# A two-layer decoder trunk on one core: the opening of layer 0, the ends of the residual and of the recurrent block, and the end of the kernel put in another order

## The chip, the cores and the metric

The kernel runs on one core of one Trainium2 chip. The metric is the device time of the whole program in microseconds (us). Before the change the median of three runs is 629.0 us (627.55 to 630.78). The weights stream in from HBM while the core computes; activations stay on the chip.

The five engines have their own instruction streams: PE (TensorE) multiplies matrices, DVE (VectorE) and ACT (ScalarE) do elementwise work, POOL (GpSimd) does a few copies, and SP (SyncE) issues the DMA transfers. PE results land in PSUM, all else in SBUF.

## The reference, cut to what matters

Batch 1, 256 positions, width 1024, float32. Two layers and a final norm:

```python
for l in range(2):
    hn  = rms_norm(h, mix_norm_g[l])
    mix = even_mixer(hn, ...) if l % 2 == 0 else odd_mixer(hn, ...)
    h   = h + mix
    h   = h + conv_ffn(rms_norm(h, ffn_norm_g[l]), ...)
return rms_norm(h, final_norm_g)

def even_mixer(x):   # layer 0: attention (8 x 64) beside gated linear attention (8 x 32 / 64)
    aq, ak, av, bq, bk, bv, bgk, bog = split(x @ w_in)
    o_a   = attention(rotary(aq), rotary(ak), av)             # causal within the 256 positions
    log_a = log_sigmoid(bgk @ w_gk2 + b_gk2) / 16             # gates of the linear attention
    o_b   = rms_norm(gla(bq * 32**-0.5, bk, bv, log_a), g) * silu(bog)
    return concat(o_a, o_b) @ w_out

def odd_mixer(x):    # layer 1: gated recurrence
    gate, xr = split(x @ w_in);  xr = causal_dwconv(xr, 4 taps)
    r, i = sigmoid(block_diag(w_a) xr + b_a), sigmoid(block_diag(w_x) xr + b_x)
    a = exp(-8 r softplus(-lam));  u = sqrt(1 - a*a) * (i * xr)
    h = scan(h_t = a_t h_(t-1) + u_t)
    return (h * gelu(gate)) @ w_out

def conv_ffn(x):     # up 1024 -> 6144, causal conv of 3 taps, u * gelu(g), down 3072 -> 1024
    u, g = split(causal_dwconv(x @ w_up, 3 taps));  return (u * gelu(g)) @ w_down
```

## The kernel before, in words

Activations lie with their channels on the 128 partitions and the 256 positions along the free axis. The residual stream h is one tile of 8 row groups (m = 0 to 7) of 128 channels. In the trace it reads `big`, the name of the buffer that it shares with the small vectors.

Every large product is done in three passes, for accuracy. A float32 operand is split into a high part of fewer bits (hi) and the rest (lo), and the product is hi·hi + hi·lo + lo·hi. The weights come in 204 chunks of 128 x 1024 (512 KB each). `issue_w` (line 120) starts the DMA of a chunk into a buffer `w`, of which there are four; ACT makes `wh` from it (line 135) and DVE makes `wl` = w − wh (line 136), and the buffer of chunk i is free for chunk i+4 when `wl` of i is done. `gemm` and `passes` (line 147) issue, for each of the 8 blocks of a chunk, three matmuls of 256 columns: wh with x hi, wh with x lo, wl with x hi. So each chunk costs ACT a wh, DVE a wl and PE 24 matmuls.

The same split is made of activations: `scaled_split` (lines 206, 207) writes X hi on ACT (`x`, an activation with the norm's gain) and X lo on DVE. The norm's 1/rms is not applied to X; it is multiplied into the products' results afterwards. `Norm.add` squares a row group (`sq`, ACT, line 173) and adds it up (`ssq`, DVE, line 180); `Norm.rstd` lets PE add over partitions (`nps`, line 188), takes the root on ACT and the reciprocal on DVE, and spreads the result with two PE transposes (line 194).

The opening of layer 0: SP issues the loads of the small vectors (`vec`), the gate weight (`wgk`), x in four pieces (`xT`), then chunks and constants. ACT and DVE make X; PE does the gate product `psg`, then the query product of the linear attention `psbq` (chunks 0 and 1), its key product `psbk` (2 and 3) and the projections of the attention `psa` (chunks 4 to 11). From psbq comes `qn`, and 16 copies on POOL (lines 387 and 390) spread it into the block forms q0 and q1; from psbk comes `kn` (DVE, line 395). DVE also makes the gates' running sums (`G`, three scans `cum`) and the factors `KR`, ACT their exponentials `E`, and DVE the products `qb` and `kb`.

`residual` (line 212) adds a product into a row group of h, squares it and splits it for the next layer. In the feed-forward block the down product `psd` of the last group (m = 7) ends the layer; the next layer's first product `psx` needs all 8 groups. In the recurrent block the function `finish` (lines 725 to 730) makes, for each of four pairs of row groups, h·gelu(gate) as hi (`r`, DVE, line 728), the same in float32 (`hh`, line 729) and lo (`r`, line 730); the product `psout` then runs over these pairs. At the end of the kernel the final norm's factor is spread by PE transposes and DVE multiplies the 8 row groups, two at a time (line 756), and SP issues four output transfers of 256 KB (line 757).

The order on each engine is set by the framework's scheduler from the program order, its own cost figures and explicit edges: `order(a, b)` makes b come after a. A list of hooks by chunk, `state["hooks"]`, lets an operation be put ahead of the wh ("h") or the wl ("l") of a given chunk. `bank` picks a PSUM tile by tag.

## Time and profile before

| | before |
|---|---|
| time, median of 3 runs | 629.0 us (627.55 to 630.78) |
| profiled execution | 628.5 us, of which the span of the profile is 626.7 us |
| PE busy | 609.1 us (97%), 5210 matmuls |
| weight loads of PE (beside its matmuls) | 594.1 us (95%) |
| DVE busy | 516.1 us (82%) |
| ACT busy | 404.2 us (64%) |
| POOL busy | 30.9 us (5%) |
| read from HBM | 109.0 MB, 176 GB/s over the span |

An engine's busy time is the time in which it executed something. Idle time is put down to what released the engine: "PE psx <- ACT x" says that a matmul into psx started when an ACT instruction that writes x had ended. The granted clock (PEclk) is the share of TensorE's full clock that it had; at 0.50 it ran at 1.2 instead of 2.4 GHz. Idle time costs something only on an engine that something later waits for; here PE is idle in few places, and these can be listed one by one.

### The profile page before, as it was taken

The page shows a single profiled execution, that of the slowest core. Times are in us where ns is not written, and L with a number is a line of the kernel's source. Part 1 is how long each engine was busy: PE and PEld are TensorE (multiplying, and loading weights), DVE is VectorE, ACT ScalarE, POOL GpSimd, SP SyncE. Part 2 cuts the span into 40 slices and gives each one's busy share as a digit, 9 for nine tenths or more (in the row PEclk, how much of TensorE's full clock was granted, in tenths as well). Part 3 has the DMA queues.
Part 4 walks back from the last instruction along what each step waited for, and adds up shares of the span by engine and source line. Part 5 has one row for each costly group of instructions (what it writes and reads, how often), then busy time and mean ns, then how long its engine had stood idle before and what let it go on. Part 6 is the DMA issues. An engine that isn't in the chain of part 4 may idle for free.

```text
span 626.7 us, 13053 instructions
## 1 busy us (share of the span) xinstructions
PE 609.1 (97%) x5210; PEld 594.1 (95%) x5210; DVE 516.1 (82%) x899; ACT 404.2 (64%) x654; POOL 30.9 (5%) x58
## 2 busy tenths in 40 slices
PE   8989999999999999999998999989999999999995
PEld 4989998999999999999998999989999999999994
DVE  6799984577999999988667859997999999986542
ACT  6796564666766677765456588966676667774310
POOL 7470000000000000000000000000000000000000
PEclk9999999999999999999999999999999999999997
DMA  8734621325755555555568504535655555556501
GB/s 306 259 105 168 210 94 68 135 101 172 235 202 202 199 202 187 192 196 198 191 219 293 177 2 167 204 137 184 220 207 201 199 202 187 187 199 202 198 5 68
DMA packets 31517, 110.91 MB, mean 177 GB/s; under 512 B 3648, under 2 KB 4192, under 8 KB 31456
## 3 DMA queue, kind: packets, MB, share of 16 engines
q1 hardware_dynamic: 31456, 110.07, 50.7%
q8 instruction: 41, 0.67, 0.4%
q14 instruction: 20, 0.16, 0.1%
HBM read 109.01 MB, written 1.05 MB: 176 GB/s over the span
## 4 chain that ended last, share of the span: by engine, by line
PE 87%; DVE 4%; DMA 4%; ACT 3%; issue 2%; SPq 0%; DVEq 0%; ACTq 0%
PE psu L147 42%; PE psd L147 17%; PE psout L147 6%; PE pst L147 4%; PE psgb L147 3%; DMA w<-w 3%; PE psx L147 3%; PE psog L147 2%; DVE wl L136 2%; PE psa L147 2%; PE psgt L147 2%; ACT wh L135 1%; PE psbq L147 1%; PE pl L463 1%; PE pss L520 1%
## 5 line engine op out<-in xcount | busy, mean ns | idle before, releaser
L135 ACT ACTIVATE wh<-w 128x1024 fp32r<-128x1024 f32 x204 | 214.3, 1060 | 141.9 <-PE psu L147 69.5
L136 DVE TENSOR_TENSOR wl<-w,wh 128x1024 fp32r<-128x1024 f32 x204 | 248.2, 1222 | 53.5 <-ACT wh L135 49.3
L147 PE MATMUL psu<-x,wh 128*128 128x256 f32 x1536 | 262.2, 276 | 0.0
L147 PEld LDWEIGHTS psu<-x,wh 128*128 128x128 f32 x1536 | 231.3, 188 | 0.0
L147 PE MATMUL psu<-x,wl 128*128 128x256 f32 x768 | 211.7, 276 | 0.0
L147 PEld LDWEIGHTS psu<-x,wl 128*128 128x128 f32 x768 | 144.1, 188 | 0.0
L147 PE MATMUL psd<-y,wh 128*128 128x256 f32 x768 | 130.5, 276 | 0.0
L147 PEld LDWEIGHTS psd<-y,wh 128*128 128x128 f32 x768 | 115.5, 188 | 0.0
L147 PE MATMUL psd<-y,wl 128*128 128x256 f32 x384 | 105.4, 276 | 0.0
L645 DVE SCALAR_TENSOR_TENSOR c<-v,big,c 128x255 f32<-128x255 f32 (+1 forms) x192 | 83.8, 477 | 0.0
L147 PEld LDWEIGHTS psd<-y,wl 128*128 128x128 f32 x384 | 71.9, 188 | 0.0
L643 ACT ACTIVATE c<-v,big 128x256 f32<-128x256 f32 x96 | 51.7, 587 | 1.0 <-DVE y L650 0.6
L638 DVE TENSOR_TENSOR v<-psu,rs 128x512 f32<-128x512 f32 x48 | 32.6, 684 | 0.0
L173 ACT ACTIVATE sq<-big 128x256 f32<-128x256 f32 x40 | 15.3, 404 | 25.3 <-DVE big L212 24.7
L147 PE MATMUL psx<-x,wh 128*128 128x256 f32 x128 | 24.2, 290 | 2.3 <-ACT x L206 2.3
L147 PE MATMUL psout<-r,wh 128*128 128x256 f32 x128 | 22.6, 279 | 2.6 <-DVE r L730 2.6
L147 PE MATMUL pst<-wh,x 128*128 128x256 f32 x128 | 24.2, 286 | 0.0
L147 PE MATMUL psa<-x,wh 128*128 128x256 f32 x128 | 22.1, 278 | 1.8 <-DVE kn L395 1.8
L147 PE MATMUL psout<-m,wh 128*128 128x256 f32 x128 | 23.4, 284 | 0.3 <-DVE m L157 0.3
L147 PEld LDWEIGHTS psx<-x,wh 128*128 128x128 f32 x128 | 20.7, 199 | 2.5 <-ACT x L206 2.5
L212 DVE TENSOR_TENSOR big<-big,psd 128x256 f32<-128x256 f32 x16 | 6.7, 420 | 19.5 <-PE psd L147 19.5
L99 ACT ACT_TABLE_LOAD x17 | 21.8, 1283 | 1.0 <-PEq L851 0.7
(200 smaller groups left out, 858.8 us busy)
## 6 DMA issues: line engine op xcount, KB each, us to landing
w<-w SPq DMA_DIRECT2D x204, 512.0 KB, 4.0
big<-xT SPq DMA_DIRECT2D x4, 256.0 KB, 3.8
out<-o SPq DMA_DIRECT2D x4, 256.0 KB, 2.4
ct<-cst SPq DMA_DIRECT2D x1, 384.0 KB, 8.0
big<-vec SPq DMA_DIRECT2D x1, 224.0 KB, 7.8
mf<-mskf SPq DMA_DIRECT2D x1, 192.0 KB, 5.1
wg<-wgk SPq DMA_DIRECT2D x1, 64.0 KB, 2.1
big<-cst SPq DMA_DIRECT2D x1, 64.0 KB, 7.5
```

Source lines behind the costliest of these rows:

```text
L99: ld = nc.scalar.preload_act_table_set(name)
L135: hi = nc.scalar.activation(wh, wt, AF.Copy)
L136: lo = nc.vector.tensor_sub(wl, wt, wh.bitcast(F32))
L147: out.append(nc.tensor.matmul(ps, a, b, start=first and i + j == 0, stop=last and i == n - 1 and j == 2, skip_group_check=skip))
L173: ins = nc.scalar.activation(sq, t, AF.Square)
L212: add = nc.vector.tensor_add(h[:, m, :], h[:, m, :], ps)
L463: nc.tensor.matmul(pv[:, :, :, cs], Kb[li, I][:, ts_], qv[:, :, :, cs], start=True, stop=True)
L520: seq.append(nc.tensor.matmul(ps[:, cs], q[r, tq * P:(tq + 1) * P], k[r, 0:(tq + 1) * P], start=False, stop=True, skip_group_check=True))
L638: nc.vector.tensor_mul(v, ps.rearrange("p (j t) -> p j t", j=2), rs[:, None, :].to_broadcast([P, 2, S]))
L643: nc.scalar.activation(c[:, j, :], v[:, j, :], AF.Identity, bias=V("fc_b", layer * 48 + ch), scale=wv(2))
L645: nc.vector.scalar_tensor_tensor(c[:, j, d:], v[:, j, 0:S - d], wv(2 - d), c[:, j, d:], op0=ALU.mult, op1=ALU.add)
```

## The change

1. **Opening, loads.** The loads of `vec` and `wgk` are issued by ACT instead of SP. SP's stream then starts with the four pieces of x. Chunks 0 and 1 are converted in halves (two wh and two wl of 512 columns).
2. **Opening, products.** The matmuls of psbq come in a fixed order: per chunk 16 with wh (x hi and x lo), then 8 with wl. The norm's last sum goes before wl of chunk 2; the key product's two halves go behind the norm's two transposes.
3. **Opening, copies.** The 16 copies into q0 and q1 go from POOL to ACT: 8 right behind qn, 8 behind the exponentials of KR.
4. **Residual ends.** The last three operations of the output projection's last group and of layer 0's feed-forward end (add, hi, lo) are put, by hooks, ahead of the wl, wh and wl of given later chunks. In the output projection's tail the first product is done in two halves of its sum over k, for both row groups in turn, and the matmuls of each tail are chained.
5. **Recurrent end.** In `finish` hi becomes an ACT copy of the float32 product, so DVE does two operations in place of three; hi of the last two pairs is put ahead of wh of chunks 131 and 132, lo of the last pair ahead of wl of chunk 129.
6. **Kernel end.** PE transposes row groups 0 to 3 of h, already multiplied by the norm's gain, into two PSUM tiles between the last down product and the last sums of the norm. ACT multiplies these two tiles by the norm's factor per position (now on the partitions), DVE multiplies groups 4 to 7 as before. The output is a flat tensor whose halves lie in two layouts.

```diff
@@ issue_w
-        hi = nc.scalar.activation(wh, wt, AF.Copy)
-        lo = nc.vector.tensor_sub(wl, wt, wh.bitcast(F32))
+        nsp = 2 if i < 2 else 1
+        for f in range(nsp):
+            cs = slice(f * CW // nsp, (f + 1) * CW // nsp)
+            hi = nc.scalar.activation(wh[:, cs], wt[:, cs], AF.Copy)
+            lo = nc.vector.tensor_sub(wl[:, cs], wt[:, cs], wh[:, cs].bitcast(F32))
@@ load_w
+    def ahead(kind, i, op):
+        state["hooks"].setdefault((kind, i), []).append(op)
+    def loaded():
+        return state["i"] - len(state["q"]) - 1
@@ out_proj, tail
-            for j in range(2):
+            groups = [(j, range(4)) for j in range(2)] if n else [(j, range(2 * i, 2 * i + 2)) for i in range(2) for j in range(2)]
...
+                    if n == 3:
+                        for kind, d, o in zip("lhl", (4, 6, 5), ops):
+                            ahead(kind, loaded() + d, o)
+            for a_, b_ in zip(mms, mms[1:]):
+                order(a_, b_)
@@ opening
-    first.append(nc.sync.dma_start(vt[:, 0:NG], vec[:, 0:NG]))
+    nc.scalar.dma_start(vt[:, 0:NG], vec[:, 0:NG])
-    first.append(nc.sync.dma_start(wg, wgk))
+    nc.scalar.dma_start(wg, wgk)
...
+    state["hooks"].setdefault(("l", 2), []).append(norm.sum)
@@ psbq
-            gemm(ps[:, hf * S:(hf + 1) * S], load_w(), X)
+            wh, wl = load_w()
...
+            mms = [mms[8 * (n % 2) + n // 2] for n in range(16)] + mms[16:]
...
-                nc.gpsimd.tensor_copy(q0[hf][r, g, :], qn[r, :])
-            for g in range(4):
-                r = slice(32 * g, 32 * g + 32)
-                nc.gpsimd.tensor_copy(q1[hf][r, :, g, :], qn[r, :].rearrange("p (a i) -> p i a", i=4))
+                nc.scalar.activation(q0[hf][r, g, :], qn[r, :], AF.Copy)
@@ psbk
-            gemm(ps[:, hf * S:(hf + 1) * S], load_w(), X)
+            mms = gemm(ps[:, hf * S:(hf + 1) * S], load_w(), X)
+            order(norm0.pe[hf][-1], mms[0])
...
+    for hf in range(2):
+        for g in range(4):
+            o = nc.scalar.activation(q1[hf][r, :, g, :], qns[hf][r, :].rearrange("p (a i) -> p i a", i=4), AF.Copy)
+            order(late, o)
@@ ffn, last residual
+                if nextg and m == KT - 1:
+                    j = loaded()
+                    for kind, d, o in zip("lhl", (9, 10, 10), add):
+                        ahead(kind, j + d, o)
@@ finish
-        nc.vector.tensor_mul(Y[:, s2, 0, :], hh[n], gb[n])
         nc.vector.tensor_mul(hh[n], hh[n], gb[n])
-        nc.vector.tensor_sub(Y[:, s2, 1, :], hh[n], Y[:, s2, 0, :].bitcast(F32))
+        hi = nc.scalar.activation(Y[:, s2, 0, :], hh[n], AF.Copy)
+        lo = nc.vector.tensor_sub(Y[:, s2, 1, :], hh[n], Y[:, s2, 0, :].bitcast(F32))
+        if n > 1:
+            state["hooks"].setdefault(("h", L1_C0 + 25 + n), []).append(hi)
+        if n == 3:
+            state["hooks"].setdefault(("l", L1_C0 + 25), []).append(lo)
@@ end of the kernel
-    rs = norm.rstd(copy=False)
-    for m in range(0, KT, 2):
+    tok = [bank("pot", "l") for _ in range(2)]
+    prev = state["last"]
+    for m in range(4):
+        for t in range(2):
+            tr = nc.tensor.transpose(tok[t][:, m * P:(m + 1) * P], h[:, m, t * P:(t + 1) * P], idt)
+            order(prev, tr)
+            prev = tr
+    rs = norm.rstd(copy=False, between=prev)
+    for i in range(2):
+        o = op.tile([P, 2 * S], F32, name="o")
+        nc.scalar.activation(o, tok[i], AF.Copy, scale=norm.tok[:, i:i + 1])
+        nc.sync.dma_start(out[:, (4 + 2 * i) * S:(6 + 2 * i) * S], o)
         o = op.tile([P, 2, S], F32, name="o")
-        nc.vector.tensor_mul(o, h[:, m:m + 2, :], rs[:, None, :].to_broadcast([P, 2, S]))
+        nc.vector.tensor_mul(o, h[:, 4 + 2 * i:6 + 2 * i, :], rs[:, None, :].to_broadcast([P, 2, S]))
```

PE at the start of psbq, before (psg is the gate product, wh0 and wl0 the parts of chunk 0):

```order
L333 MATMUL psg_228<-x_102,gw_75 32x256
L147 MATMUL psbq_299<-x_102,wh0_85 128x256 x2
L147 MATMUL psbq_299<-x_102,wl0_86 128x256
L147 MATMUL psbq_299<-x_102,wh0_85 128x256 x2
L147 MATMUL psbq_299<-x_102,wl0_86 128x256
L147 MATMUL psbq_299<-x_102,wh0_85 128x256 x2
```

PE at the same place, after (wh1, wl1 and wh2 belong to chunks 1 and 2, nps is the norm's sum):

```order
L355 MATMUL psg_232<-x_104,gw_75 32x256
L410 MATMUL psbq_303<-x_104,wh0_85 128x256 x16
L410 MATMUL psbq_303<-x_104,wl0_86 128x256 x8
L410 MATMUL psbq_303<-x_104,wh1_160 128x256 x16
L410 MATMUL psbq_303<-x_104,wl1_161 128x256 x8
L199 MATMUL nps_253<-big_70,ssq_149 128x1 x2
L157 MATMUL psbk_365<-x_104,wh2_168 128x256 x2
```

The triples wh, wh, wl became 16 matmuls with wh and then 8 with wl, for each of the two chunks; the sum of the norm follows them directly.

DVE around kn, before (G and cum are the gates' sums, rotq0 the rotary form of the query, psa its product):

```order
L136 TENSOR_TENSOR wl10_616<-w10_613,wh10_615 128x1024
L358 SCALAR_TENSOR_TENSOR G_278<-z_270,az_271 128x512
L363 SCALAR_TENSOR_TENSOR cum64_177<-cum64_177,G_278 128x512
L363 SCALAR_TENSOR_TENSOR cum16_180<-cum16_180,G_278 128x512
L363 SCALAR_TENSOR_TENSOR cum4_183<-cum4_183,G_278 128x512
L136 TENSOR_TENSOR wl11_656<-w11_653,wh11_655 128x1024
L395 TENSOR_TENSOR kn_368<-psbk_369,rs_257 128x512
L404 TENSOR_TENSOR KR64_433<-cum64_177 128x512
L404 TENSOR_TENSOR KR16_436<-cum16_180 128x512
L404 TENSOR_TENSOR KR4_439<-cum4_183 128x512
L490 TENSOR_TENSOR rotq0_508<-psa_442,ct_172 128x512
```

DVE at that place, after:

```order
L381 SCALAR_TENSOR_TENSOR G_282<-z_274,az_275 128x512
L146 TENSOR_TENSOR wl13_731<-w13_728,wh13_730 128x1024
L386 SCALAR_TENSOR_TENSOR cum64_181<-cum64_181,G_282 128x512
L386 SCALAR_TENSOR_TENSOR cum16_184<-cum16_184,G_282 128x512
L386 SCALAR_TENSOR_TENSOR cum4_187<-cum4_187,G_282 128x512
L525 TENSOR_TENSOR rotq1_582<-psa_516,ct_176 128x512
L526 TENSOR_TENSOR rt2_577<-rt2_577,ct_176 128x512
L146 TENSOR_TENSOR wl14_737<-w14_734,wh14_736 128x1024
L470 TENSOR_TENSOR qb_1071<-q0_0_216,E64_285 128x1024
L425 TENSOR_TENSOR kn_364<-psbk_365,rs_261 128x512
L434 TENSOR_TENSOR KR64_429<-cum64_181 128x512
L434 TENSOR_TENSOR KR16_432<-cum16_184 128x512
```

kn stands behind the scans in both. Before, one wl stands between the scans and kn; after, the rotary product of the second query half, wl14 and a qb do, and wl12 and wl13 are ahead of the scans.

DVE at the end of the recurrent block, before (the numbers 2 and 3 of uu, hh and gb are the last two pairs; r is the product's operand):

```order
L136 TENSOR_TENSOR wl130_5449<-w130_5446,wh130_5448 128x1024
L723 SCALAR_TENSOR_TENSOR hh2_4515<-aa2_4503,uu2_4507 128x512
L720 TENSOR_TENSOR uu3_4508<-tt3_4512,ii3_4500 128x512
L728 TENSOR_TENSOR r_4525<-hh2_4515,gb2_4519 128x2x256
L723 SCALAR_TENSOR_TENSOR hh3_4516<-aa3_4504,uu3_4508 128x512
L729 TENSOR_TENSOR hh2_4515<-hh2_4515,gb2_4519 128x512
L728 TENSOR_TENSOR r_4525<-hh3_4516,gb3_4520 128x2x256
L730 TENSOR_TENSOR r_4525<-hh2_4515,r_4525 128x2x256
L136 TENSOR_TENSOR wl131_5493<-w131_5490,wh131_5492 128x1024
L729 TENSOR_TENSOR hh3_4516<-hh3_4516,gb3_4520 128x512
L136 TENSOR_TENSOR wl132_5537<-w132_5534,wh132_5536 128x1024
L136 TENSOR_TENSOR wl133_5601<-w133_5598,wh133_5600 128x1024
```

DVE there, after:

```order
L759 TENSOR_TENSOR uu2_4511<-tt2_4515,ii2_4503 128x512
L762 SCALAR_TENSOR_TENSOR hh2_4519<-aa2_4507,uu2_4511 128x512
L759 TENSOR_TENSOR uu3_4512<-tt3_4516,ii3_4504 128x512
L762 SCALAR_TENSOR_TENSOR hh3_4520<-aa3_4508,uu3_4512 128x512
L767 TENSOR_TENSOR hh2_4519<-hh2_4519,gb2_4523 128x512
L767 TENSOR_TENSOR hh3_4520<-hh3_4520,gb3_4524 128x512
L769 TENSOR_TENSOR r_4529<-hh2_4519,r_4529 128x2x256
L769 TENSOR_TENSOR r_4529<-hh3_4520,r_4529 128x2x256
L146 TENSOR_TENSOR wl129_5411<-w129_5408,wh129_5410 128x1024
L146 TENSOR_TENSOR wl130_5453<-w130_5450,wh130_5452 128x1024
L146 TENSOR_TENSOR wl131_5497<-w131_5494,wh131_5496 128x1024
L146 TENSOR_TENSOR wl132_5541<-w132_5538,wh132_5540 128x1024
```

The two r = hh·gb of DVE are gone (ACT makes them), and wl129 to wl132, which stood among or ahead of the last steps, follow the last lo.

## Rows read from the trace of the kernel before

**Rows 1.** The page: busy time by engine.

```profile
PE 609.1 (97%) x5210; PEld 594.1 (95%) x5210; DVE 516.1 (82%) x899; ACT 404.2 (64%) x654; POOL 30.9 (5%) x58
```

**Rows 2.** PE's waits in the span: us in total, times, longest.

```profile
PE psout L147 <- DVE r L730: 2.6, 2, 1.5
PE psx L147 <- ACT x L206: 2.3, 1, 2.3
PE psa L147 <- DVE kn L395: 1.8, 1, 1.8
...
PE psbq L147 <- ACT wh L135: 0.9, 1, 0.9
...
PE psbq L147 <- DVE wl L136: 0.8, 1, 0.8
```

**Rows 3.** Busy time by stretch, PE, PEld, DVE, ACT, POOL; then PEclk, DMA.

```profile
13.00:16.00 3.00, 3.00 (x16) 3.00 (x15) 2.90 (x5) 1.27 (x5) 1.75 (x4) 0.50 1.05 395
...
20.00:30.00 10.00, 10.00 (x82) 9.36 (x82) 7.84 (x10) 8.37 (x13) 5.20 (x4) 1.00 0.72 243
30.00:40.00 10.00, 8.22 (x72) 8.05 (x72) 9.52 (x9) 8.18 (x16) 9.58 (x10) 1.00 0.52 165
40.00:60.00 20.00, 20.00 (x169) 19.67 (x168) 20.00 (x36) 16.24 (x26) 3.42 (x4) 1.00 0.38 129
60.00:80.00 20.00, 20.00 (x164) 18.44 (x164) 19.93 (x47) 9.35 (x19) 0.00 (x0) 1.00 0.61 207
```

**Rows 4.** Timeline of the opening: start, length, instruction [idle before <- releaser].

```profile
0.73 1.28 ACT L99 ACT_TABLE_LOAD   x1 [0.73 <-PEq L851]
...
0.73 0.38 SPq L253 DMA_DIRECT2D big<-vec  x1
...
1.64 1.85 SPq L260 DMA_DIRECT2D big<-xT  x4
...
5.23 3.30 ACT L206 ACTIVATE x<-big 128x256 fp32r<-128x256 f32 x8 [1.63 <-DMA big<-xT]
...
11.72 0.38 PE L147 MATMUL psbq<-x,wl 128*128 128x256 f32 x1 [0.76 <-DVE wl L136]
```

**Rows 5.** DMA issues of the first 14 us: KB each, median us to landing.

```profile
big<-xT SPq DMA_DIRECT2D x4, 256.0 KB, 3.8
...
big<-vec SPq DMA_DIRECT2D x1, 23.0 KB, 1.7
```

**Rows 6.** PE's timeline, 22 to 40 us: the first attention projection.

```profile
26.28 0.51 PE L147 MATMUL psa<-x,wh 128*128 128x256 f32 x2
```

**Rows 7.** DVE, 24 to 44 us, by form: busy, mean ns, idle before.

```profile
L136 DVE TENSOR_TENSOR wl<-w,wh 128x1024 fp32r<-128x1024 f32 x5 | 6.3, 1285 | 1.0 <-ACT wh L135 1.0
L363 DVE TENSOR_TENSOR_SCAN cum<-cum,G 128x512 f32<-128x512 f32 x3 | 4.3, 1471 | 0.1
```

**Rows 8.** The same forms of DVE, whole span and 44 to 80 us.

```profile
L723 DVE TENSOR_TENSOR_SCAN hh<-aa,uu 128x512 f32<-128x512 f32 x4 | 4.9, 1217 | 0.0
...
L136 DVE TENSOR_TENSOR wl<-w,wh 128x1024 fp32r<-128x1024 f32 x12 | 14.5, 1210 | 0.0
```

**Rows 9.** POOL's copies, 20 to 44 us, by form.

```profile
L387 POOL COPY q<-qn 32x256 f32<-32x256 f32 x8 | 9.4, 1174 | 8.7 <-DVE qn L384 8.4
```

**Rows 10.** ACT's nearest forms: squares (the page), rotary copies (24 to 60 us).

```profile
L173 ACT ACTIVATE sq<-big 128x256 f32<-128x256 f32 x40 | 15.3, 404 | 25.3 <-DVE big L212 24.7
...
L488 ACT ACTIVATE rt<-psa 32x512 f32<-32x512 f32 x16 | 9.4, 590 | 0.2
```

**Rows 11.** Timeline at the end of layer 0, ACT and DVE.

```profile
340.66 1.06 ACT L135 ACTIVATE wh<-w 128x1024 fp32r<-128x1024 f32 x1 [1.01 <-DMA w<-w]
...
340.83 0.41 DVE L212 TENSOR_TENSOR big<-big,psd 128x256 f32<-128x256 f32 x1
```

**Rows 12.** DVE's timeline at the end of the recurrent block.

```profile
412.40 0.68 DVE L730 TENSOR_TENSOR r<-hh,r 128x512 fp32r<-128x512 f32 x1
```

**Rows 13.** Timeline of the last 10 us.

```profile
620.72 2.48 DVE L756 TENSOR_TENSOR o<-big,nps 128x512 f32<-128x512 f32 x4 [0.58 <-PE nps L194]
```

More of the change, by code (lines that the diff above doesn't have):

```diff
@@ L179, in add, with rstd @@
                 n = tp.tile([P, S], F32, tag="ssq", name="ssq")
-                nc.vector.tensor_add(n, self.acc.pop(), sq)
+                self.sum = nc.vector.tensor_add(n, self.acc.pop(), sq)
                 self.acc.append(n)
             self.m += 1
-        def rstd(self, copy=True, hook=0):
+        def rstd(self, copy=True, hook=0, between=None):
             ps = bank("nps", "t")
+            sums = []
             for t in range(2):
                 for i, s_ in enumerate(self.acc):
-                    nc.tensor.matmul(ps[:, t:t + 1], s_[:, t * P:(t + 1) * P], ones, start=i == 0,
-                                     stop=i == len(self.acc) - 1)
+                    sums.append(nc.tensor.matmul(ps[:, t:t + 1], s_[:, t * P:(t + 1) * P], ones, start=i == 0,
+                                                 stop=i == len(self.acc) - 1))
+            if between:
+                order(between, sums[len(self.acc) - 1])
             rt = tp.tile([P, 32], F32, tag="rtk", name="rtk")[:, 0:2]
@@ L192, in rstd @@
             inv = nc.vector.reciprocal(rt, rt)
-            for t in range(2):
-                nc.tensor.transpose(ps[:, S + t * P:S + (t + 1) * P], rt[:, t:t + 1].to_broadcast([P, P]), idt)
-            self.tok = rt
+            trs = [nc.tensor.transpose(ps[:, S + t * P:S + (t + 1) * P], rt[:, t:t + 1].to_broadcast([P, P]), idt)
+                   for t in range(2)]
+            self.tok, self.pe = rt, (sums, trs)
             if not copy:
@@ L214, in residual @@
         if X is not None:
-            scaled_split(X, m, h[:, m, :], V(gname, gi * KT + m))
-        return add
+            return (add,) + scaled_split(X, m, h[:, m, :], V(gname, gi * KT + m))
+        return add, None, None
     def out_proj(M):
@@ L380, in trunk @@
         for hf in range(2):
-            gemm(ps[:, hf * S:(hf + 1) * S], load_w(), X)
+            wh, wl = load_w()
+            mms = []
+            for a, i in ((wh, 0), (wh, 1), (wl, 0)):
+                for k in range(KT):
+                    mms.append((a[:, k * P:(k + 1) * P], X[:, k, i, :]))
+            mms = [mms[8 * (n % 2) + n // 2] for n in range(16)] + mms[16:]
+            seq = [nc.tensor.matmul(ps[:, hf * S:(hf + 1) * S], a, b, start=n == 0, stop=n == 23)
+                   for n, (a, b) in enumerate(mms)]
+            for a_, b_ in zip(seq, seq[1:]):
+                order(a_, b_)
         for hf in range(2):
```

34 lines of the change are left out of this document (21 added, 13 removed).

## The prediction

> **What bounds the kernel now.** I read the busy times first, then PE's list of waits, then the stretches, and only then the timelines of the places where PE waits. PE is busy 609.1 of 626.7 us [rows 1]; the reader is to see that no engine can be relieved for a general gain, and that only PE's holes, its slow clock and the head and tail can be shortened. The list of waits says where: 2.6 us at the end of the recurrent block, 2.3 at the start of layer 1, 1.8 on kn in the opening, 0.9 and 0.8 at the first product psbq [rows 2]. The stretches add two things. From 13 to 16 us PE is full, but with 16 matmuls in 3 us at a granted clock of 0.50, the lower of its two levels; from 60 to 80 us 164 matmuls took 20 us [rows 3]. So the slow stretch costs about 3.0 − 16 x 20/164 = 1.05 us, and up to 1.5 with the neighbouring instants. Second, from 40 to 80 us DVE is busy 39.9 of 40 us [rows 3]: what PE gains before this stretch, DVE must follow.
>
> I go by the profiled execution, 628.5 us (span 626.7 and 1.8 around it), 0.5 below the median of 629.0. About 0.5% (3.1 us) is what can be told from no change; the bounds are 625.9 and 632.1.
>
> **Opening: loads and first product.** ACT's first x waits 1.63 us for the x pieces and starts at 5.23 [rows 4]. SP issues them from 1.64 on; without vec (0.73) and wgk ahead they go out 0.91 earlier [rows 4]. But vec now leaves ACT after its table load, which ends at 0.73 + 1.28 = 2.01. The old vec load landed in 1.7 us, an xT piece in 3.8 [rows 5], so vec lands between 3.7 and 5.8, and x starts between 4.3 and 5.8: −0.9 to +0.6. I take −0.6 (vec is small, so nearer 1.7). The Trainium skill speaks against more: in "DMA: Bandwidth & Descriptors", section "Issuing engines are not separate DMA queues", it says that transfers from several engines share the same 16 DMA engines, and that only issue time is saved. By that rule vec still shares them with xT and the start is nearer +0.6; no run here shows which.
>
> psbq in the old order runs two matmuls, waits for wl, and runs freely only from 11.72 [rows 4]. Now 16 matmuls with wh go first, 16 x 0.12 = 1.9 us of work, which covers wl. The waits of 0.9 and 0.8 go [rows 2]; with the earlier x that is about −2.2. What is late next is each wh half, an ACT step of about half a microsecond against 1 us of PE work. If PE does not pause there, the slow stretch may vanish too: −1.5, or nothing. The first attention product psa starts at 26.28 now [rows 6]; 22.6 with all of this. The wait on kn, 1.8, goes as well: kn is made later than before in DVE's order, but by the assignment of PSUM tiles it is no longer psa that reuses psbk's tile, but a later product (pst). PE could thus be 2.2 + 1.5 + 1.9 = 5.6 us ahead at the end of psa.
>
> **Opening: what DVE and ACT allow.** DVE's operations until 80 us are the same but for two chunks in halves. So DVE can be ahead by what it stops losing. (a) Its earlier start, 0.6. (b) Slower operations beside POOL's copies: wl takes 1285 ns there against 1210, a scan of 128 x 512 1471 against 1217 [rows 7, 8]; (75 x 5 + 254 x 3) ns = 1.1 us. POOL's 16 copies take some 1.17 us each [rows 9] and go. The Trainium skill has a rule for this ("SBUF — State Buffer", section "SBUF: two separate sides"): a DVE operation with two SBUF inputs and a GpSimd operation that reads SBUF exclude each other for a whole instruction. By it each such DVE operation could lose a whole copy, 1.17; the rows show 0.08 to 0.25 each, so I keep 1.1. (c) Idle time in 20 to 40 us, 10.0 − 7.84 + 10.0 − 9.52 = 2.6 [rows 3], of which some two thirds, 1.8, should go, since wh comes earlier. Together 3.5. PE does not wait from 40 to 80 us, so it keeps no more than DVE's lead and what slack it had: 3.5 is what I take, between 0.6 (only the start counts) and 5.6.
>
> The 16 copies fall to ACT. A square of 128 x 256 takes 404 ns there, a rotary copy of 32 x 512 590 ns [rows 10]: 6.5 to 9.4 us. From 20 to 60 us ACT is free 40 − (8.37 + 8.18 + 16.24) = 7.2 us [rows 3]. By the first price it fits; the copies have 256 columns, so I take that one. If the cover is gone, wh comes late and DVE and PE wait.
>
> **Output projection of layer 0.** None of the five waits above lies there; the halved sums and hooks change the order of work that PE does not wait for. 0, between −0.3 and +1.0.
>
> **Start of layer 1.** PE waits 2.3 us for x of the last row group [rows 2]. On ACT that x follows a wh which starts at 340.66, held for 1.01 us by its chunk's DMA; the add on DVE starts at 340.83, behind a wl [rows 11]. After the change this wh and this wl still stand ahead of them: the hooks only move x ahead of a chunk that ACT had already done earlier. The wait stays. Another wl now lies between the add and the last lo, 1.2 us; PE has matmuls to fill most of it. I take +0.3, between −3.8 (2.3 and 1.5 of slow clock gone) and +1.2.
>
> **End of the recurrent block.** lo of the last pair starts at 412.40 [rows 12]. Ahead of it go four wl (1.21 each) and two products (0.68 each): 6.2 us earlier if DVE alone set it. But hi is now ACT's, two copies of 0.59 and a wh of 1.06 in the chain, so about 4 us earlier. The 2.6 us of waits [rows 2] end. What is late next is wl129 to wl132, which now follow lo and hold their buffers, so the loads of the next four chunks start some 8 us later; and the first lo of the feed-forward block follow those wl. I expect 1.8 of the 2.6 given back there: −0.8, between −2.6 and 0.
>
> **End of the kernel.** Four multiplications on DVE take 2.48 us from 620.72 [rows 13]. Two remain, 1.24; ACT does two beside them (1.2 by the rotary copies) without waiting for the transposes. The eight new transposes lie in PE's wait for the last square. The last multiplication ends 1.24 earlier, but four transfers of 256 KB share the DMA engines whenever they start: −0.7, between −0.2 and −1.2.
>
> **Sum.** 628.5 − 3.5 + 0 + 0.3 − 0.8 − 0.7 = 623.8.
>
> **Rivals.**
> - *DVE takes the lead back.* DVE's 39.9 busy us of 40 [rows 3] speak for it; against it, that it was slowed and idle in the stretch before. The opening then gives its earlier start only: 628.5 − 0.6 + 0.3 − 0.8 − 0.7 = 626.7.
> - *ACT becomes the bound in the opening* (the one on the other side). At 590 ns the 16 copies cost 9.4 us, 2.2 more than ACT has free. Each wh behind them comes later, and PE with it: +2.2 instead of −3.5, so 628.5 + 2.2 + 0.3 − 0.8 − 0.7 = 629.5. It decides from 7.2/16 = 0.45 us a copy on for the opening, and from (7.2 + 1.2)/16 = 0.53 for the whole. For it: 32-partition forms are no cheaper on ACT than 128 x 512 ones. Against: half the columns.
> - *The start of the next feed-forward block starves* for the four chunks loaded late: one chunk of PE work (24 matmuls, 2.9 us) lost in place of −0.8: 628.5 − 3.5 + 0.3 + 2.9 − 0.7 = 627.5.
> - *All of the lead is kept*, PE's slack covering DVE: 628.5 − 5.6 + 0.3 − 0.8 − 0.7 = 621.7.
>
> **How the numbers follow.** The forecast 0.50, with its own range 621.9 to 625.9; DVE takes it back 0.20; ACT becomes the bound 0.10; starved 0.08; all of it kept 0.12. Faster by over 0.5% (below 625.9): 0.48 of the forecast, 0.12, and 0.03 of the first rival, 0.63. Within 0.5%: 0.32. Slower: 0.05, if a copy costs over 0.75 us. The range reaches from the last rival less 1.2, 620.5, to 629.0, half of the ACT rival left out.
>
> **What would show it.** Opening: psbq without waits from about 9.7; PEclk above 0.50 in the next stretch; psa from about 22.6; no wait on kn; PE waits of 1 to 3 us in total between 50 and 80, on wl. ACT's q copies near 0.4 us. Layer 1: a wait of about 2.3 on x again. Recurrent end: the waits on r below 0.5, new ones on wl or x soon after. End: the last transfer issued about a microsecond sooner after the last square. It is wrong if PE's waits between 50 and 80 us exceed 4 us, if the q copies cost over half a microsecond, or if the wait at layer 1 is gone.

## The result, and the profile after

| | before | after |
|---|---|---|
| time, median of 6 runs each | 629.1 us (627.6 to 631.0) | 623.4 us (621.6 to 626.1) |
| profiled execution (span) | 628.5 (626.7) | 622.7 (620.9) |

The ratio of the times is 0.991, with a 95% interval of 0.988 to 0.993: 5.7 us or 0.9% faster. The forecast was 623.8.

The page of the changed kernel, busy time by engine, answers to [rows 1]:

```profile
PE 607.5 (98%) x5218; PEld 595.1 (96%) x5218; DVE 508.0 (82%) x895; ACT 416.3 (67%) x678; POOL 13.6 (2%) x42
```

PE's busy time fell by 1.6 only, its span by 5.8: the gain is holes and slow stretches, not work. DVE lost 8.1 us, POOL 17.3, ACT gained 12.1. PE's list of waits, to be held against [rows 2] (us in total, times, longest):

```profile
PE psx L157 <- ACT x L219: 2.2, 1, 2.2
PE warm L290 <- POOL wz L287: 1.4, 1, 1.4
PE psout L157 <- ACT r L768: 1.0, 1, 1.0
PE psg L355 <- DVE gw L279: 0.8, 1, 0.8
PE psu L157 <- ACT wh L145: 0.6, 1, 0.6
...
PE psbq L410 <- ACT wh L145: 0.5, 1, 0.5
```

The wait on kn is gone, the one on r fell from 2.6 to 1.0, psbq's two fell from 1.7 to 0.5 (it now starts at 9.64), and the one on x at layer 1 stayed. The stretches of the opening answer to [rows 3] (busy time of PE, PEld, DVE, ACT, POOL, then PEclk and DMA):

```profile
13.00:16.00 3.00, 3.00 (x29) 2.95 (x28) 2.79 (x6) 1.99 (x6) 2.22 (x4) 1.00 1.01 383
...
20.00:30.00 10.00, 10.00 (x81) 9.48 (x80) 6.47 (x10) 8.76 (x16) 0.00 (x0) 1.00 0.71 239
30.00:40.00 10.00, 10.00 (x86) 10.00 (x86) 8.75 (x10) 9.83 (x15) 0.00 (x0) 1.00 0.74 249
40.00:60.00 20.00, 20.00 (x167) 19.43 (x167) 20.00 (x33) 19.72 (x34) 0.00 (x0) 1.00 0.32 114
60.00:80.00 20.00, 19.88 (x169) 18.89 (x170) 20.00 (x55) 13.73 (x34) 0.00 (x0) 1.00 0.61 211
```

In 13 to 16 us PE does 29 matmuls instead of 16, at the upper clock. PE does not wait from 20 to 60 us. DVE is full from 40 to 80 as before, but from 20 to 40 it has more idle time than before (4.8 us instead of 2.6), not less. The chain up to the first attention product reads so in the timeline (start, length, instruction, idle before and releaser), against [rows 4, 6]:

```profile
0.76 0.39 ACTq L274 DMA_DIRECT2D big<-vec  x1
...
4.47 1.88 ACT L219 ACTIVATE x<-big 128x256 fp32r<-128x256 f32 x4 [2.46 <-DMA big<-vec]
...
9.64 2.15 PE L410 MATMUL psbq<-x,wh 128*128 128x256 f32 x16 [0.49 <-ACT wh L145]
...
22.84 0.51 PE L157 MATMUL psa<-x,wh 128*128 128x256 f32 x2
```

psa, the first attention product, starts at 22.84, where it was 26.28. From the starts and ends of PE's products in the two profiled executions, the difference by stage:

| stage, by PE | before | after | difference |
|---|---|---|---|
| start to the output projection of layer 0 | 113.8 | 108.1 | −5.7 |
| from there to the end of layer 0's feed-forward | 222.4 | 222.9 | +0.5 |
| layer 1: to the end of its gate products | 59.8 | 59.2 | −0.6 |
| end of the recurrent block (to the first psu) | 25.0 | 24.0 | −1.0 |
| feed-forward of layer 1, its psu (to its first psd) | 131.4 | 132.9 | +1.5 |
| its psd and the end of the kernel | 74.3 | 73.8 | −0.5 |

The column adds up to the 5.8 us between the spans. Nearly all of the gain is the opening, and layer 1 from its start on moves the time by less than a microsecond in all. Some 1.2 us of the opening's gain hang on the half clock from 13 to 16 us, which not every execution of the old opening has: in *copies on ACT alone* (experiment 2), where the opening is the old one up to there, PEclk stays at 1.00 and psa starts at 25.10 instead of 26.28.

### The profile page after: what moved, and what is told of

Same layout as the page of the kernel before. It is cut to its first block, busy times and chain, and to the rows that moved or that the text cites. A ratio compares the mean times of both kernels' runs of the same rounds, so it can differ in the third digit from the quotient of the medians.

```text
span 620.9 us, 13046 instructions
## 1 busy us (share of the span) xinstructions
PE 607.5 (98%) x5218; PEld 595.1 (96%) x5218; DVE 508.0 (82%) x895; ACT 416.3 (67%) x678; POOL 13.6 (2%) x42
## 4 chain that ended last, share of the span: by engine, by line
PE 78%; ACT 10%; DMA 5%; DVE 4%; issue 1%; DVEq 0%; SPq 0%; ACTq 0%
PE psu L157 42%; PE psd L157 17%; DMA w<-w 4%; ACT wh L145 4%; PE psa L157 4%; PE pst L157 4%; PE psout L157 3%; ACT L99 2%; DVE wl L146 2%; PE psog L157 1%; DVE xc L724 1%; PE psbq L410 1%; PE psbk L157 1%; DMA big<-xT 1%; ACT tt L108 1%
## 5 line engine op out<-in xcount | busy, mean ns | idle before, releaser
L145 ACT ACTIVATE wh<-w 128x1024 fp32r<-128x1024 f32 (+1 forms) x206 | 214.9, 1051 | 133.6 <-PE psu L157 67.0
L146 DVE TENSOR_TENSOR wl<-w,wh 128x1024 fp32r<-128x1024 f32 (+1 forms) x206 | 248.6, 1212 | 56.1 <-ACT wh L145 53.0
L157 PE MATMUL psout<-r,wh 128*128 128x256 f32 x128 | 22.6, 280 | 1.1 <-ACT r L768 1.0
```

The costliest lines, as they stand in the source:

```text
L145: hi = nc.scalar.activation(wh[:, cs], wt[:, cs], AF.Copy)
L146: lo = nc.vector.tensor_sub(wl[:, cs], wt[:, cs], wh[:, cs].bitcast(F32))
L157: out.append(nc.tensor.matmul(ps, a, b, start=first and i + j == 0, stop=last and i == n - 1 and j == 2, skip_group_check=skip))
```

## The experiments

The experiments were timed in three groups, each beside the kernel before, whose medians there are 628.7 us (runs of *opening only*, *copies back on POOL*, *x ahead of four*, *roots first*), 629.9 (*opening and tail*, *copies on ACT alone*, *psbq in triples*, *both mends*) and 628.9 (the rest). The ratios are to the kernel before of the same group. So a difference of about a microsecond against the changed kernel, or between groups, is not told from nothing.

**1. The opening alone, and with the residual's tail.** In *opening only* the edits to `finish`, the kernel's end, the two hooks at the residual's ends and the reordered tail are taken back; parts 1 to 3 of the change stay. In *opening and tail* the tail and its hook are there too.

```diff
 opening only, against the changed kernel:
-            groups = [(j, range(4)) for j in range(2)] if n else [...halves...]
+            groups = [(j, range(4)) for j in range(2)]
-                        for kind, d, o in zip("lhl", (4, 6, 5), ops): ahead(...)
-            for a_, b_ in zip(mms, mms[1:]): order(a_, b_)
 opening only, and opening and tail:
-                    for kind, d, o in zip("lhl", (9, 10, 10), add): ahead(...)
 ... finish and the kernel's end as before
```

> The changed opening (loads, psbq, copies) with all later edits undone. Theory 1 (the opening alone made the gain, and the edits at the later ends about cancel): output projection of layer 0 starts near 108.1 us as in the changed kernel (113.8 before), waits on x at layer 1 (2.3) and on r (2.6) stand as before; time 5.0 to 5.8 us below before, so about the changed kernel's. Rival (the sizes of the prediction: opening 3.5, the ends 1.2): 3.5 us below before, 2 us above the changed kernel.

> The changed opening and the changed tail of the output projections, the other later edits undone. In the run with the opening alone the output projection of layer 0 was as early as in the changed kernel (108.0), but from 139.9 to 279.2 us PE started a matmul every 118.7 ns in place of 113.3, at a granted clock of 1.00 and without a wait, and the first product of the feed-forward block took 137.2 in place of 131.8 us. Theory 1 (that spacing is a state which the order of work at the end of the output projection sets; with the tail edits PE's order up to layer 1 is the changed kernel's word for word): spacing 113.3 from 152 us on, that product 131.8 us, time near 623. Rival (it comes from something else, as the placing of later tiles or code): spacing 118.7 again, time near 628.4.

Opening only: 628.4 us, ratio 1.000 (0.998 to 1.002). Its output projection starts at 108.0, as early as in the changed kernel, so the opening's gain is there. It is lost afterwards: psu of layer 0 takes 137.2 us, from its start to the first psd, where the changed kernel takes 131.8 and the one before 131.4. PE waits nowhere in it, its clock is granted in full, and yet it does fewer matmuls in the same time. Two stretches of *opening only*:

```profile
150.00:170.00 20.00, 20.00 (x170) 20.00 (x170) 20.00 (x35) 14.01 (x24) 0.00 (x0) 1.00 0.73 231
170.00:190.00 20.00, 20.00 (x171) 20.00 (x170) 19.46 (x35) 13.33 (x22) 0.00 (x0) 1.00 0.58 198
```

The same stretches of *opening and tail*:

```profile
150.00:170.00 20.00, 20.00 (x178) 20.00 (x177) 19.98 (x37) 14.37 (x24) 0.00 (x0) 1.00 0.58 189
170.00:190.00 20.00, 20.00 (x179) 20.00 (x179) 20.00 (x36) 14.33 (x24) 0.00 (x0) 1.00 0.62 209
```

From start to start this is 118.7 ns instead of 113.3 (a stretch also counts the matmuls that its ends cut). The slow spacing lasts from 139.9 to 279.2 in *opening only* and costs 137.2 − 131.8 = 5.4 us. All ten timed runs of this kernel lie between 627.7 and 632.3, so the loss is not a matter of the profiled one. Opening and tail: 622.5 us, ratio 0.989 (0.984 to 0.993), psu of layer 0 in 132, with waits of 3.1 on x and 2.1 on r. So the opening's gain is real and the slow spacing ate it; and the rest of the change (`finish`, the hook, the kernel's end) adds nothing that can be measured to *opening and tail* (622.5 against 623.4).

**2. The copies back on POOL, and the copies on ACT in the old kernel.**

```diff
 copies back on POOL, against the changed kernel:
-                nc.scalar.activation(q0[hf][r, g, :], qn[r, :], AF.Copy)
+                nc.gpsimd.tensor_copy(q0[hf][r, g, :], qn[r, :])
+            ... (q1 by nc.gpsimd.tensor_copy, and the ACT loop behind KR gone)
 copies on ACT alone, against the kernel before: the same edit the other way round
```

> The changed kernel with its 16 copies into q0 and q1 back on POOL. Theory 1 (beside POOL's copies DVE's operations are slower by 3.3 us in all, and the lead of 5.6 us was kept because this loss went): scans of 128x512 back at 1.4 to 1.5 us, the output projection 2 to 3 us later than in the changed kernel, time +2 to +3. Rival (PE's lead was kept because PE has other work to fill with and DVE had slack): DVE's operations slower all the same, output projection within 0.7 us, time within 0.7 of the changed kernel; the copies gone from ACT give nothing either.

> The kernel before with nothing changed but the 16 copies, put on ACT as in the change. Theory 1 (POOL's copies cost DVE 3.3 us beside them): scans back to 1.2 us, the wait on kn shorter by a microsecond or gone, output projection of layer 0 2 to 3 us earlier, time 1.5 to 3 us below before. Rival (the copies delay the gates on ACT by 3.4 us, and kn stands behind the gates' scans): the wait on kn grows to 3 us or more, output projection no earlier, time 0 to 3 us above before.

Copies back on POOL: 624.9, ratio 0.994 (0.992 to 0.996). The output projection starts at 112.7, 4.6 later than in the changed kernel; 4.1 of this is a new wait of PE, `pst <- rotq`, on DVE. DVE by form from 20 to 50 us (busy, mean ns, idle before):

```profile
L468 DVE TENSOR_TENSOR qb<-q,E 128x1024 f32<-128x1024 f32 x4 | 5.6, 1441 | 0.0
L386 DVE TENSOR_TENSOR_SCAN cum<-cum,G 128x512 f32<-128x512 f32 x3 | 4.4, 1504 | 0.1
L437 DVE TENSOR_TENSOR KR<-cum 128x512 f32<-128x512 f32 x3 | 2.6, 905 | 0.0
L524 DVE TENSOR_TENSOR rt<-rt,ct 128x512 f32<-128x512 f32 x2 | 1.4, 676 | 0.0
L523 DVE TENSOR_TENSOR rotq<-psa,ct 128x512 f32<-128x512 f32 x2 | 1.3, 668 | 0.0
```

In the changed kernel the same view has:

```profile
L386 DVE TENSOR_TENSOR_SCAN cum<-cum,G 128x512 f32<-128x512 f32 x3 | 3.4, 1204 | 0.0
L434 DVE TENSOR_TENSOR KR<-cum 128x512 f32<-128x512 f32 x3 | 1.9, 682 | 0.0
...
L470 DVE TENSOR_TENSOR qb<-q,E 128x1024 f32<-128x1024 f32 x1 | 1.2, 1216 | 0.0
```

DVE is slower beside POOL's copies. But its order changed with the edit too: here kn, the three KR and all four qb stand ahead of the second rotq product of psa, which starts at 48.85; in the changed kernel they all follow it (42.43). The run shows what both cost together, 4.6 us, and does not separate them.

The time is only 1.5 above the changed kernel's, since there is no wait on x at layer 1 in this run (55.3 us for that stage instead of 59.2): 4.6 lost there, 1.3 more up to the end of layer 0, 3.9 given back.

Copies on ACT alone: 627.5, ratio 0.997 (0.995 to 1.000). DVE is as quick as in the changed kernel (scan 1209 ns, KR 684), but the output projection starts at 114.0, no earlier than before. PE's list has instead:

```profile
PE psa L147 <- ACT E L108: 2.7, 1, 2.7
```

The third product psa waits, as it did for kn [rows 2]; E and kn end at the same instant here (38.81) and psa reads neither, so the trace does not tell this wait from the old one. psa starts 1.2 us earlier than before, and that is lost again: as the rival has it, the gates come later with ACT's copies ahead of them (G starts at 32.84 instead of 31.76). Moving the copies alone gave the opening nothing.

**3. What holds psa: the order of psbq, and kn's place.** In the kernel before, the third psa product takes the PSUM tile in which psbk stood, so it waits until kn has read it. In the changed kernel, by the assignment of tiles in the program, that tile next goes to the second pst; the trace does not number the tiles, but shows kn as late as 45.88 and no wait of the third psa product, which starts near 34.4. In *psbq in triples* the old order of psbq's matmuls and the whole chunks are put back; with that the tile goes to psa again. In the two kernels *kn early* the gates' chain is moved behind kn in the program, so that DVE makes kn first.

```diff
 psbq in triples, against the changed kernel:
-        nsp = 2 if i < 2 else 1
+        nsp = 1
-            mms = [mms[8 * (n % 2) + n // 2] for n in range(16)] + mms[16:]
-            ...
+            gemm(ps[:, hf * S:(hf + 1) * S], load_w(), X)
 kn early, against psbq in triples and against the kernel before:
-        psz = bank("psz", "t")
-        ... (z, G, the three scans, E)
         nc.vector.tensor_mul(kn, ps, rs)
+        psz = bank("psz", "t")
+        ...
```

> The changed kernel with psbq in triples again and chunks 0 and 1 converted whole. Theory 1 (the new order removed the waits of 0.9 and 0.8 us and, with them, the three microseconds at half clock): waits of 1 to 2 us on wh and wl at psbq, granted clock near 0.5 for some 3 us before 18 us, psa starts 2.5 to 3.5 us later than in the changed kernel (22.8); if PE's lead is kept, time +2 to +3. Rival (DVE is full from 40 to 80 us and sets the pace): psa later all the same, but the output projection within 1 us of the changed kernel and the time with it.

> The kernel of the run with psbq in triples (632.6 us, a wait of 9.0 us on kn), with kn early in the same way. Theory 1 (that run lost by the PSUM tile that psa took over from psbk, not by the order of psbq): the wait of 9 us is gone, psa starts near 24.3 and the output projection near 110, time 624 to 625.5, 1 to 2 us above the changed kernel: that is what the order of psbq is worth. Rival (the order of psbq matters by itself): the time stays over 628.

> The kernel before with one thing moved: the gates' chain (psz to E) is written behind kn, so that kn stands on DVE behind wl8 and ahead of the scans. Theory 1 (the wait of 1.8 us on kn is the reuse of psbk's PSUM tile by a product of psa, and nothing else): the wait is gone, the output projection of layer 0 starts 1.5 to 2 us earlier than in the kernel before (113.8), time 1.5 to 2 us below before. Rival (DVE, full from 40 to 80 us, takes it back): the wait is gone and the output projection within 0.5 us.

psbq in triples: 632.6, ratio 1.004 (1.002 to 1.007), slower than before. PE's list and two of its stretches:

```profile
PE psa L157 <- DVE kn L416: 9.0, 1, 9.0
```

```profile
13.00:16.00 3.00, 3.00 (x29) 3.00 (x28) 2.76 (x6) 1.44 (x4) 2.08 (x4) 1.00 1.04 404
...
35.00:45.00 10.00, 1.03 (x9) 0.82 (x7) 10.00 (x13) 6.20 (x11) 0.00 (x0) 0.77 0.39 140
45.00:50.00 5.00, 4.96 (x23) 4.99 (x24) 5.00 (x8) 4.96 (x11) 0.00 (x0) 0.50 0.00 0
```

kn at 44.2 holds psa for 9 us, and behind the wait PE runs at half its clock. The half clock from 13 to 16 us did not come back with the triples and their waits on wh and wl (0.9 and 0.8); *copies on ACT alone*, whose opening up to 16 us is the old one, hasn't it either (28 matmuls at 1.00). So the triples and their waits are not enough to cause it. *kn early* in the kernel before, with the old opening as well, has the half clock again:

```profile
13.00:16.00 3.00, 3.00 (x16) 3.00 (x16) 3.00 (x4) 1.30 (x4) 1.94 (x3) 0.50 1.04 384
```

Of the three profiled executions of the old opening two have it, of the nine with psbq in the new order none. What decides it is open.

With kn early beside the triples the 9 us are gone: 623.6, ratio 0.992 (0.989 to 0.994), output projection at 109.7. psa does not read kn, so the wait can only have come through the PSUM tile, and the order of psbq itself is worth at most 109.7 − 108.1 = 1.6 us in the opening and nothing in the total. In the kernel before, kn early takes the wait away and gains nothing: 628.4, ratio 0.998 (0.996 to 1.001); DVE, still beside POOL's copies, is late for the next products, and the output projection starts at 115.9 (1.5 us of that stand ahead of psa, which starts at 27.83 in this profile instead of 26.28, with the half clock):

```profile
PE pa L442 <- DVE kb L419: 1.7, 1, 1.7
```

So the opening seems to have had two limits one behind the other, psbk's tile and DVE beside POOL. Neither edit alone gave a gain clear of the noise. That nothing else takes part is argued: the copies also load ACT and change DVE's order, and both lifted in the old opening was not tried.

**4. The wait at layer 1.** In *x ahead of four* the add, hi and lo of the last residual are hooked ahead of the wh and wl of four chunks in turn, so that they stand ahead of the first of them too.

```diff
-                    for kind, d, o in zip("lhl", (9, 10, 10), add):
-                        ahead(kind, j + d, o)
+                    for kind, o in zip("lhl", add):
+                        for d in range(9, 13): ahead(kind, j + d, o)
```

> The changed kernel, with add, hi and lo of the last row group of layer 0 put ahead of the wl and wh of four chunks (112 to 115) in place of one. Theory 1 (the wait of 2.25 us at layer 1 stands because x follows a wh that waits for its chunk's DMA, and the slow clock behind it, 1.7 us, is a consequence of the wait): both go, time 3 to 4 us below the changed kernel. Rival (something else is late next: the four chunks held back are missed by the next product or their DMA): the wait reappears on wh within 20 us, time within 1 us of the changed kernel.

619.7, ratio 0.985 (0.983 to 0.988). The stretch of the changed kernel, and then of this one:

```profile
334.00:337.00 3.00, 0.99 (x9) 0.79 (x7) 2.28 (x3) 2.37 (x4) 0.00 (x0) 1.00 0.06 20
337.00:340.00 3.00, 2.76 (x13) 2.77 (x14) 3.00 (x5) 1.67 (x3) 0.00 (x0) 0.50 0.80 259
```

```profile
334.00:337.00 3.00, 3.00 (x29) 3.00 (x28) 3.00 (x4) 2.98 (x5) 0.00 (x0) 1.00 0.39 135
337.00:340.00 3.00, 3.00 (x29) 3.00 (x28) 1.91 (x3) 1.68 (x2) 0.00 (x0) 1.00 0.92 264
```

In this pair the wait of 2.2 us and the 3 us at half clock behind it go together: 58 matmuls in 6 us instead of 22. A wait does not always bring the half clock: with kn early beside the triples PE waits 2.0 us for the same x, and PEclk stays at 1.00 from 334 to 346. The hooks of the changed kernel named one wh and one wl too far back.

**5. The end of the recurrent block.** In *roots first* the square roots of pairs 2 and 3 are put ahead of wh129, and hi of these pairs ahead of wh129 and wh130 instead of wh131 and wh132. In *finish as before* part 5 of the change alone is undone.

```diff
 roots first, against the changed kernel:
-            act(SQRT, tt[n], tt[n], AF.Sqrt, scale=-1.0)
+            root = act(SQRT, tt[n], tt[n], AF.Sqrt, scale=-1.0)
+            if n > 1: state["hooks"].setdefault(("h", L1_C0 + 25), []).append(root)
-            state["hooks"].setdefault(("h", L1_C0 + 25 + n), []).append(hi)
+            state["hooks"].setdefault(("h", L1_C0 + 23 + n), []).append(hi)
 finish as before: the lines of finish in the change, the other way round
```

> The changed kernel; at the end of the recurrent block the two last square roots and the two last hi copies stand on ACT ahead of wh of chunks 129 and 130. Theory 1 (the remaining wait on r, 1.0 us, and the wait on wh at the start of the feed-forward block, 0.6, come from ACT's order: DVE waits 2.5 us for the root behind a wh): both waits go, feed-forward block of layer 1 starts 1 to 1.5 us earlier relative to the recurrent block, time 1 to 2 us below the changed kernel. Rival (the waits only move: wh129 and wh130 come late and PE waits for them): PE waits 1 us or more on wh or wl in psout, time within 0.5.

> The changed kernel with the recurrent block's finish as before (hi and lo on DVE, no hooks there). Theory 1 (that edit won nothing: the waits of 2.6 us became 1.0 and 0.6, and the first product of the feed-forward block of layer 1 took 132.9 in place of 131.4 us): time within 0.7 us of the changed kernel, waits on r of 2 to 2.7 us, that product 131.5 us. Rival (the prediction's 0.8): time 0.8 to 1.5 us above the changed kernel.

Roots first: 622.5, ratio 0.990 (0.987 to 0.993). The wait on r is gone, but PE's list has `psu <- x` 1.6 in its place, and psu of layer 1 takes 135.7 instead of 132.9. In part this is because its first matmuls now start ahead of psout's last (411.28 and 413.14); from the last gate product to the first psd it is 156.2 us instead of 156.9. So 0.7 to 0.9 gained at best, which the intervals don't separate from nothing.

Finish as before: 631.3, ratio 1.003 (1.001 to 1.005), 7.9 above the changed kernel and missed by both expectations. Three things show in its profile. The waits on r are longer than they were even in the kernel before:

```profile
PE psout L157 <- DVE r L769: 2.8, 1, 2.8
...
PE psout L157 <- DVE r L767: 0.8, 1, 0.8
```

Behind the longer one PE runs near half its clock for some 3 us, which the changed kernel does not have here:

```profile
406.90:410.90 4.00, 4.00 (x23) 4.00 (x23) 1.97 (x2) 0.00 (x0) 0.00 (x0) 0.59 0.76 253
```

(27.7 us from the gate products to psu, instead of 24.0.) And psu of layer 1 takes 136.9, at the slow spacing from 430 to 564:

```profile
435.00:455.00 20.00, 20.00 (x171) 20.00 (x170) 20.00 (x37) 13.56 (x23) 0.00 (x0) 1.00 0.59 192
```

**6. Both mends together.** *Both mends* is *x ahead of four* with *roots first*; *both mends, kn early* has kn ahead of the gates' chain as well.

```diff
 the two edits above, in one kernel (and for the second one the move of the gates' chain)
```

> The changed kernel with both mends: x of the last row group ahead of four chunks, and roots and hi copies of the recurrent block ahead of wh of chunks 129 and 130. Theory 1 (the two are independent): 619.7 less 0.9, 618 to 619.3. Rival (PE's spacing of 118.7 ns takes the place of what is won): 620 or more with 131.5 us of the feed-forward block of layer 1 grown to 134 or more.

> The kernel with both mends, 618.6 us, and kn early as well. Theory 1 (its opening has no wait on kn left, so nothing is to be won): 618 to 619.5. Rival (kn early relieves DVE's order behind it, or sets PE's spacing anew): over 1 us away from 618.6 either way.

Both mends: 618.6 (618.0 to 618.9), ratio 0.982 (0.979 to 0.985), the lowest median of all: 11.3 us below the kernel before of its group and 4.9 below the changed one. The 1.1 below *x ahead of four* alone lies within the intervals. Its longest waits outside the head and the tail are

```profile
PE psu L157 <- DVE x L220: 1.0, 2, 0.8
...
PE pl L502 <- DVE m L167: 0.5, 1, 0.5
```

With kn early too: 620.2, ratio 0.985 (0.982 to 0.988), 1.6 above, which the intervals don't separate from nothing. In the profile the output projection starts at 109.8 instead of 108.1, of which 0.65 stand ahead of psa (23.17 and 22.52), and `pl <- m` is 1.1. So kn early wins nothing once psa doesn't need the tile; that kn then holds up other work of DVE is argued.

## Why the prediction was right, step by step

The time is where the forecast put it, and most changes of place are those named; but the terms are off by up to 2 us each and their errors partly cancel. The opening gave 5.7 instead of 3.5, all that follows it 0.1 instead of 1.2. That the sum came out so near is in part luck.

- **Opening, start.** x starts 0.76 earlier (forecast 0.6), for another reason: ACT's queue issues vec at 0.76 while the table load still runs, not after it at 2.01. It lands 3.6 us after its issue, beside the xT pieces, where it took 1.7 ahead of them [rows 5], and ACT waits for it. The Trainium skill's rule in "DMA: Bandwidth & Descriptors", section "Issuing engines are not separate DMA queues", agrees: the second issuing engine saved issue time, and the transfer itself shared the engines and took twice as long.
- **Opening, psbq.** Free from 9.64 with 0.5 of wait and psa at 22.84 (forecast 9.7 and 22.6): right. That the half clock of 13 to 16 us would go was right for the profiled pair, but *psbq in triples* and *copies on ACT alone* lack it with the waits still there, so the cause given (PE's pauses on wh and wl) does not hold by itself. As it comes and goes in the old opening, the 1.5 us taken for it were not certain to be won.
- **Opening, kn.** Right that the wait goes: no psa waits in the changed kernel, though kn is made 7.5 us later than before (45.88 and 38.43). *psbq in triples* and its mend show what the tile can cost, 9 us. That it is pst which takes the tile over rests on the assignment in the program.
- **Opening, DVE's lead: the step that was wrong.** The forecast kept 3.5 of the 5.6 us that PE would be ahead (a sum with 1.9 for kn, where the row has 1.8): no more than DVE's lead, one number for all of its work, and PE's slack, which it put at nothing. 5.7 came at the output projection, the size of the rival "all of the lead is kept". The traces, counted by chunks (eight of PE's matmuls with wl for each), show both parts otherwise. wl of chunks 12 to 15 is done 6 to 12 us earlier than before, since DVE's new order has these wl ahead of the gates' work. wl of chunks 16 to 21 is done only 2.2 to 2.9 us earlier, and there PE's slack gives way. wl of chunk 16 and PE's first matmul with it, before:

```profile
57.37 1.21 DVE L136 TENSOR_TENSOR wl<-w,wh 128x1024 fp32r<-128x1024 f32 x1
...
63.88 0.28 PE L147 MATMUL pst<-wl,x 128*128 128x256 f32 x1
```

And after:

```profile
54.63 1.22 DVE L146 TENSOR_TENSOR wl<-w,wh 128x1024 fp32r<-128x1024 f32 x1
...
58.05 0.28 PE L157 MATMUL pst<-wl,x 128*128 128x256 f32 x1
```

It was ready 5.3 us ahead of its use and is now 2.2 ahead: DVE gained 2.7 us and PE 5.8. The two terms that the lead was added up from were off in opposite directions. (b) was put at 1.1; from 20 to 50 us of both kernels DVE's forms give 3 x 267 ns for the scans, 3 x 308 for KR, 434 for G, 4 x 107 for qb, 8 x 42 for wl and some 0.4 for two ct, 3.3 us. The forecast looked at two forms only. (c), 1.8 of DVE's idle time going, was wrong in sign: from 10 to 80 us DVE idles 6.3 instead of 4.2. The waits of 1 to 3 us on wl between 50 and 80 did not come.

- **The copies on ACT.** 8 into q0 at 414 ns and 8 into q1, reading qn with a stride, at 668 make 8.7 us, where 6.5 were forecast; by the forecast's own test (it decides from 0.45 us a copy in the opening, 0.53 for the whole; measured 0.54) the ACT rival should have come true, and copies of over half a microsecond were one of its signs of being wrong. It did not come: ACT is busy 19.72 of 20 us from 40 to 60, and nothing on PE waits for it there. That the copies are part of what made the gain is what experiment 2 shows, with DVE's changed order mixed in.
- **Output projection of layer 0.** +0.5 to the end of layer 0, forecast 0 with +1.0 at most. In *opening only* the slow spacing came without the tail's edits and went with them; but the kernel before has none of these edits and no slow spacing in its feed-forward blocks either, so the tail's order does not decide it by itself.
- **Start of layer 1.** The wait stayed, 2.2, as forecast, and *x ahead of four* shows the reason given (wh and wl left ahead of the three operations) and the price (3.7 us in the medians, with the half clock). The stage came out at −0.6 instead of +0.3; by which step is open.
- **End of the recurrent block.** −0.8 was forecast as 2.6 less 1.8 given back. Up to psu it gained 1.0, and psu of layer 1 took 1.5 longer, 0.6 of it the wait on wh. In five profiled runs with the old `finish` at the normal spacing (before, *opening only*, *opening and tail*, *copies on ACT alone*, *kn early* in the kernel before) it is 131.2 to 131.4 us from the last psout to the first psd, in the eight with the new one 132.7 to 133.9. So more was given back than forecast: from the last gate product to the first psd the changed kernel takes 156.9 us, the kernel before 156.4 and *opening and tail*, which differs there by `finish` alone, 155.7 (the five old ones 155.7 to 156.7, the five new ones without *roots first* 156.7 to 157.9). By these profiles the step won nothing and cost some 0.5 to 1.2 us. The mechanism that the forecast named shows: wl129 to wl132 start at 404.10, no DMA runs from 398.2 to 406.2, and wh133 waits 4.46 us for its chunk. That it is the whole of the loss was not tried alone. *Finish as before* does not answer it cleanly, as the slow spacing and a half clock came with it.
- **End of the kernel.** From the last psd to the end 8.3 us instead of 8.8: −0.5, forecast −0.7. The last transfer is issued at 617.00, and ACT's two multiplications take 1.27 us beside DVE's 1.28.

The rivals: DVE did not take the lead back; ACT was fuller than thought and still no bound; the next feed-forward block lost 1.5, not 2.9; all of the lead was kept, by the slack that this rival names.

## What to carry to other kernels

When one engine is busy all the time, ask how far ahead of its use its work is done: such slack lets the engine behind it come closer before it waits. Where an engine waits for a value that frees a PSUM tile, look which product takes that tile next: an unrelated reorder can hand it to another one, and that decided 9 us here. Two limits one behind the other can show no gain when lifted singly, so a null result for one edit is no verdict on the pair. Hook an operation ahead of the first queued step that may be in its way, not ahead of one that is expected to be there.

## What the runs showed of the hardware

- **Two spacings of PE at the full granted clock.** Without waits and at PEclk 1.00 PE does 179 or 171 matmuls of 256 columns in 20 us, one each 113.3 or 118.7 ns. The slow spacing came over whole feed-forward blocks in *opening only* (139.9 to 279.2, psu 137.2) and *finish as before* (430 to 564, psu 136.9), some 5 us each. The changed kernel's attention products run at it too (87 matmuls in each 10 us from 24 to 44, some 119 ns from start to start), where the kernel before does 91 from 27 to 37. The DMA traffic goes neither way (in 150 to 170 and 170 to 190 231 and 198 GB/s in the slow block, 189 and 209 in the fast one), and neither has waits. What sets it is open.
- **The half clock is no fixed consequence of a pause.** The same old opening, with the same two waits, had 16 matmuls at PEclk 0.50 from 13 to 16 us in two profiled executions and 28 at 1.00 in a third.
- **POOL's copies and DVE's operations hold each other up.** KR went from 682 to 990 ns, the scans from 1204 to 1471, wl from 1218 to 1260; operations that read PSUM did not change (kn 683 and 676). The Trainium skill ("SBUF — State Buffer", section "SBUF: two separate sides") has a lock between a DVE operation with two SBUF inputs and a GpSimd operation that reads SBUF, held for a whole instruction. The trace agrees in both directions. No such operation lost more than 0.47 us (a scan in *copies back on POOL* took 1671 ns, where they take 1204 in the changed kernel), about the length of POOL's shortest copies, and the longest copy, 3.9 us in the kernel before, lies beside three wl that ran back to back from 25.87 and lost nothing:

```profile
L387 POOL COPY q<-qn x8: 398/853/3902, 24.7 to 38.8; 32x256 f32<-32x256 f32 x8
```

(Shortest, median and longest, in ns; spans on POOL are rough.) So the mean of 1.17 us that the forecast took for a copy holds POOL's own waits. Not every such operation loses: rt, with two SBUF inputs, took 676 ns beside the copies and 680 without, each time behind an operation that reads PSUM.

- **The form of an ACT copy counts.** The same 32 x 256 elements took 414 ns copied in order and 668 when every fourth element was read and the result written in rows of 64.
